# A hybrid decoder block in seven-product form: the output product's weights loaded and summed during the projections, and the attention branch's turned heads emptied a step ahead

## The chip, the cores and the metric
The kernel runs on one core of a Trainium2 chip. The metric is the device time of one execution in microseconds (us). Its engines are TensorE (PE in the profile, PEld its weight loads), VectorE (DVE), ScalarE (ACT), GpSimd (POOL) and SyncE (SP), which only issues DMAs here. Each engine works through its own instructions in the order in which they stand in the program, and waits on semaphores for the others.

## The reference, cut to what matters
One layer, 1024 positions, width 1024, all in float32. Two branches work on the normalised input and meet in gates; an MLP follows.

```python
h = rms_norm(x, g_mix)
z = h @ w_in                      # q1 q2 k1 k2 v | qr kr vr gr | gate_a gate_t
a = diff_attention(q1, q2, k1, k2, va, lam)            # 4 heads of 128
a = _rms(a, SUBLN_EPS) * g_diff_sub * (1 - lam_init)
r = _rms(retention(qr, kr, vr), ...) * silu(gr)        # 4 heads of 128
m = sigmoid(gate_a) * (a @ w_diff_proj) + sigmoid(gate_t) * (r @ w_ret_proj)
x = x + m @ w_out
u = causal_dwconv(rms_norm(x, g_ffn) @ w_up, conv_w, conv_b)
x = x + (silu(gate half of u) * (other half)) @ w_down
out = rms_norm(x, g_final)
```

The lines are shortened: shapes and reshapes are left out.

## The kernel before
**Numbers in two pieces.** Every float32 operand of a product is cut into an upper piece `hi` and a remainder `lo`, both fp32r: ScalarE makes `hi` (`copy`, line 291), VectorE makes `lo` (`sub`, line 285). One product of two such operands is three matmuls: hi with hi, hi with lo, lo with hi (`part`, line 276). A tile of a `Form` holds `hi` in its columns 0 to 511 and `lo` behind it.

**Seven products for eight.** A product of two matrices cut in four quadrants each is done with seven smaller products, of sums of quadrants. For the output product `wo` (`m @ w_out`) the parts run in the order 1, 6, 5, 7, 3, 4, 2. Each part goes over four k (128 rows of a quadrant) and, within a k, over four blocks d of 128 output channels, three matmuls for each k and d: 12 a k, 48 a part. Parts 1, 6, 7, 4 gather in one set of four PSUM banks (tag a), parts 5, 3, 2 in another (tag b). With u0, u1 the left and right half of a weight tile `wou` and v0, v1 those of `wov` (in the trace's names), the weight sides of the parts are: 1: u0; 6: S2 = v1 - S3; 5: S1 = u1 + v1; 7: S3 = u0 - u1; 3: v0 - S2; 4: v1; 2: v0. `Loaded.prepare` (line 1026) makes the sums, `Loaded.side` (line 1034) hands them out. Before, S3 is written over u0 and S1 over u1, just ahead of the parts that use them.

**The stages around the change.** In the program's order: the last gates (`gt`, a product of the normalised input, ending about 582 us); in their last steps the four heads of the attention's result `oa` are turned; the projection `pa` of the attention (eight weights `wpa`, 24 matmuls each); the projection `pr` of the retention (eight weights `wpr`, the same); the output product `wo`; the norm; the MLP's two products (`up`, `wd`).

**The steps.** The stages are written as a list of `Step`s, and `issue` (line 338) writes the program from it. At step i it issues the loads of step i + 9, the sums of step i + 4, the `hi` copies of step i + 3, the `lo` remainders of step i + 2, and then the step's own `pre` list, its matmuls `mm` and its `post` list (evictions and whatever was hung on the step):

```python
(0, lambda s: s.first), (LOAD, lambda s: s.load), (SUMS, lambda s: s.sums), (HI, ...),
(LO, ...), (0, lambda s: s.pre + [s.mm] + s.post),
```

`at_step(i, op)` hangs an operation on the end of step i's `post`; `load_with(i, op)` has a load issued during step i. The projections and `wo` stand in the order in which this writes them; `n_gates` is the number of steps up to the end of the gates, and every weight of `pa` and `pr` has two steps (its two halves of 512 columns).

**Turned heads.** `turn_a(h)` (line 795) transposes the eight 128 x 128 blocks of head h into two PSUM banks (`turned`, line 783, tag "b", two banks in all; `pta` in the trace). `finish_a(h)` empties them: two ScalarE copies for the upper piece (line 803), two VectorE operations for the remainder (line 805). Head h is turned at the end of step n_gates - 7 + h and was emptied at the end of the next step, behind that step's evictions. The next head's transposes, which need the same two banks, stand behind that.

**Projections.** `projection` (line 758) loads a weight `raw_pa` or `raw_pr` (SP's queue), splits it, and runs two steps of 12 matmuls. `times` (line 918) multiplies each half into the loaded gate (`ga_in`, `gt_in`; line 922, VectorE); `merge` (line 966) adds the two branches (line 288) and, for blocks 4 to 7, makes the three sums `t` and `ga_in` that the output product's activations need (line 285).

**Queues and tiles.** All loads here are issued by SP in one order (`Queue.load`, line 171: each is ordered behind the one before). SP waits at a load until the tile that it fills is free, and what is behind it waits too. Tiles come from tags with a fixed number of buffers each; a new tile takes the oldest buffer of its tag, once its last reader is done. Before, the sixteen quarter loads of `wo` (256 KB each) stand behind all loads of the projections, in the order u0, u1, v0, v1 over the four k, then the eight blocks of `x2` (the residual input), and `zg` and `zu` weights follow. `evict_wo` adds each part to `x2` (line 288) and each finished half is saved by another SP transfer.

Of the kernel before, what the change touches and what calls it, by code (L numbers as in the profile page):

```python
# [135 lines left out]
def hybrid_block(ctx: ExitStack, tc: tile.TileContext, units, xT, wall, lams, pars, consts, dist, out):  # L136
# [6 lines left out]
    def t4(tag, name, dt=F32, shape=(P, 1024)):  # L143
        return tp.tile(list(shape), dt, tag=tag, name=name, bufs=BUFS[tag])
# [35 lines left out]
    queue = Queue()  # L180
# [101 lines left out]
    HK = KB // 2  # L282

    def sub(out, a, b, engine=nc.vector):
        engine.tensor_tensor(out, a, b, op=ALU.subtract)  # L285

    def plus(out, a, b, engine=nc.vector):
        engine.tensor_tensor(out, a, b, op=ALU.add)  # L288
# [24 lines left out]
    def weight_form(src, name):  # L313
        n_forms[0] += 1
        return Form(("whi", "wlo")[n_forms[0] % 2], src, name)
# [10 lines left out]
    steps, index, behind = [], {}, []  # L326
# [23 lines left out]
    def manual():  # L350
        return tc.manual_schedule(engines={getattr(mybir.EngineType, n) for n in ("PE", "DVE", "Activation", "Pool")})

    with ExitStack() as first:
# [13 lines left out]
        u = []  # L367
        w = None
        for k in range(KB):
            xt = t4("s", f"x{k}")  # L370
            tag = "br" if k < 4 else "c" if k < 6 else "vo" if k < 7 else "s"
# [57 lines left out]
        for h in range(NH):  # L429
            for c in range(2):  # L430
                v = va[h][:, 4 * c : 4 * c + 4, :]
# [168 lines left out]
        class Pair:  # L600
# [20 lines left out]
            def add(self, p):  # L621
                side = {1: "a11", 2: "a12", 5: "a21", 6: "s2", 7: "a11", 3: "a12", 4: "a22"}[p]
                w = weight_form(lambda: getattr(self, side), f"w{self.label}_{p}")
                into_a = p in (1, 6, 7, 4)

# [115 lines left out]
        def at_step(i, *ops):  # L741
            steps[i].post.extend(ops)

        def load_with(i, *ops):

            steps[i + LOAD].load[:0] = ops

        def act_step(label, ps, w, acts, c, load=(), forms=(), post=()):

            cs = slice(c * 512, (c + 1) * 512)  # L750

            def mm():
                ps[c] = psum("gx", f"ps_{label}_{c}")
                part(ps[c], [(w.t, k * P) for k in range(NH)], [[t[:, cs] for t in acts[k]] for k in range(NH)], True, True)

            step((label, c), mm, load, (), forms, [partial(op, cs, lambda: ps[c]) for op in post])

        def projection(name, j, acts, load, done, behind=()):

            raw, ps = {}, {}  # L760

            def load_raw():
                raw[0] = t4("wraw", f"raw_{name}{j}")[:, 0:512]
                queue.load_unit(raw[0], (name, j))

            w = weight_form(lambda: raw[0], f"w{name}_{j}")
            for c in range(2):
                act_step(
                    f"{name}{j}", ps, w, acts, c, [load_raw, *load] if c == 0 else (), [w] if c == 0 else (),
                    [lambda cs, ps: done(cs, ps())],  # L770
                )
            steps[-1].post.extend(behind)
# [6 lines left out]
        def scale_heads(o, r):  # L779

            nc.vector.tensor_tensor(o, o, r.rearrange("p (a b) -> p a b", b=1).broadcast_to([P, 8, DV]), op=ALU.mult)
# [113 lines left out]
        n_gates = len(steps)  # L895
# [7 lines left out]
        for h in range(NH):  # L903
            at_step(18 + h, lambda h=h: scale_heads(oa[h], rstd_a[:, h * NST : (h + 1) * NST]))
            at_step(n_gates - 7 + h, partial(turn_a, h))
            at_step(n_gates - 6 + h, partial(finish_a, h))


        MERGED = ("br",) * 5 + ("s", "s", "vo")
# [8 lines left out]
        def times(t):  # L918


            def go(cs, ps):
                nc.vector.tensor_tensor(t()[:, cs], t()[:, cs], ps, op=ALU.mult)

            return go
# [32 lines left out]
        for n in range(2 * NH):  # L957
            h, c = n // 2, n % 2
# [16 lines left out]

        for j in (0, 4, 1, 5, 2, 6, 3, 7):
            projection("pr", j, rT, [partial(load_gate, j)], times(lambda j=j: gates[j]), [partial(merge, j)])
        with manual():
            issue(4)

# [39 lines left out]
    class Loaded(Resident):  # L1020
# [3 lines left out]
            return []  # L1024

        def prepare(self, p, k):
            if p == 6:
                self.sum2(k)
            if p == 5:
                self.sum1(k)  # L1030
            if p == 3:
                sub(self.s24[k], self.tiles[1][k][:, 0:512], self.s24[k])

        def side(self, p, k):
            u, v = (t[k] for t in self.tiles)
            s = self.s24.get(k)
            return {1: u[:, 0:512], 7: u[:, 0:512], 2: v[:, 0:512], 4: v[:, 512:], 6: s, 3: s, 5: u[:, 512:]}[p]

    class Streamed(Resident):

# [126 lines left out]
    tc.keep_in_program_order(nc.scalar.activation(table, eps_n, AF.Sqrt))  # L1167
    steps.clear()
    index.clear()
    wo = Loaded("wo", ["g", "wraw", "wraw", "h0"], ["h0"] * HK, "h0")  # L1170
    for q in (0, 2, 1, 3):
        for k in range(HK):
            wo.load(k, q)
    for d in range(KB):
        x2.append(t4("h1" if d < HK else "s", f"x2_{d}"))
        x2_saved.append(dram.tile([P, S], F32, name=f"x2_saved{d}"))
# [15 lines left out]
    def evict_first(p, d, ps, cols):  # L1192
# [8 lines left out]
    seven_parts(  # L1201
        "wo", (1, 6, 5, 7, 3, 4, 2), HK, wo, lambda p, k: [],
        lambda p, k: [partial(merged_sum4, k)] if p == 4 else [], merged_side,
        lambda p, k: "h0" if p == 1 and k < 2 else "c",
        evict_first, squared_wo, {p: (2, [slice(0, 512)]) for p in (3, 4, 2)},
    )

# [379 lines left out]
```

## Time and profile before

| | before |
|---|---|
| median of 3 runs | 1434.86 us (1434.17 to 1435.17) |
| profiled execution | 1434.84 us |
| its span | 1433.0 us |
| mean granted TensorE clock | 0.984 of full |
| TensorE busy | 1368.6 us, 96% |
| VectorE busy | 1068.0 us, 75% |
| ScalarE busy | 703.4 us, 49% |
| GpSimd busy | 154.3 us, 11% |

The span is that of the profiled execution, from its first instruction to its last; the time reported for it is 1.84 us longer. Busy times are sums over the whole span, so they say which engine is scarce, not where. Where time is lost is read from the waits and the timelines of single stretches: a row of a timeline is a run of like instructions with its start, its length and, in brackets, the idle time ahead of it and the operation of another engine that ended it. `PEclk` in a table of stretches is the granted TensorE clock as a share of full speed. Buffer numbers are left out of the names: `wpr` is any of the eight split weights of that name.

### The profile page before, as it was taken

To read this page: it belongs to the slowest core of one execution; us is meant where nothing else is said; L and a number is where in the kernel's file an instruction comes from. 1 tells how busy PE (TensorE), PEld (TensorE's weight loads), DVE (VectorE), ACT (ScalarE), POOL (GpSimd) and SP (SyncE) were. 2 spreads that over 40 slices of the span, in tenths; PEclk is the share of its full clock that TensorE was granted. 3 is DMA by queue.
4 is the path that set the end of the run, shared out by engine and by line. 5 is a ranking of instruction groups with operands and counts; after the bars stand their busy time and mean duration, and the time that the engine had idled before them with its cause. 6 is when DMAs were issued, how large, how long until landed. Compare 5 with 4: busy or idle time off the path is not lost.

```text
span 1433.0 us, 18055 instructions
## 1 busy us (share of the span) xinstructions
PE 1368.6 (96%) x6472; PEld 1134.0 (79%) x6472; DVE 1068.0 (75%) x1699; ACT 703.4 (49%) x1318; POOL 154.3 (11%) x92
## 2 busy tenths in 40 slices
PE   7899899989999998999998989999999999999996
PEld 7887788878888886788776767888888888888885
DVE  6759765675655553467968989888988899897876
ACT  6544665564454434221445465455555556444452
POOL 6711001000000000000000012111111112200000
PEclk9999999999999999999989999999999999999997
DMA  7313101314334332635324134434433365943223
GB/s 250 125 45 121 56 16 45 137 70 143 137 125 136 108 110 81 251 138 180 153 100 148 59 113 159 133 122 136 139 126 125 125 228 195 331 165 103 94 90 118
DMA packets 81018, 187.55 MB, mean 131 GB/s; under 512 B 8320, under 2 KB 18944, under 8 KB 80928
## 3 DMA queue, kind: packets, MB, share of 16 engines
q1 hardware_dynamic: 80736, 185.74, 37.8%
q8 instruction: 51, 0.84, 0.2%
q0 software_dynamic: 192, 0.66, 0.1%
q14 instruction: 39, 0.32, 0.1%
HBM read 136.81 MB, written 49.55 MB: 130 GB/s over the span
## 4 chain that ended last, share of the span: by engine, by line
PE 42%; DVE 7%; ACT 1%; issue 1%; DVEq 0%; ACTq 0%
PE up L276 24%; PE wd L276 14%; PE wo L276 4%; DVE wf L285 1%; DVE f L285 1%; DVE x L1461 1%; DVE y L1381 1%; DVE ssum L228 1%; DVE x L1230 1%; DVE x L288 1%; DVE x L285 0%; ACT f L291 0%; DVE zg L288 0%; DVE raw_zg L285 0%; DVE wwo L285 0%
## 5 line engine op out<-in xcount | busy, mean ns | idle before, releaser
L276 PE MATMUL up<-f,wf 128*128 128x512 f32 x1848 | 424.8, 391 | 9.2 <-DVE wf L285 3.4
L276 PEld LDWEIGHTS up<-f,wf 128*128 128x128 f32 x1848 | 345.3, 188 | 88.1 <-DVE wf L285 6.4
L276 PE MATMUL wd<-awd,wwd 128*128 128x512 f32 (+1 forms) x960 | 212.2, 383 | 0.0
L276 PEld LDWEIGHTS wd<-awd,wwd 128*128 128x128 f32 x960 | 176.0, 189 | 35.4 <-issue 0.5
L285 POOL TENSOR_TENSOR t12g<-y 128x512 f32<-128x512 f32 x11 | 19.8, 1796 | 673.3 <-DVE y L1391 538.4
L276 PE MATMUL wo<-awo,wwo 128*128 128x512 f32 x336 | 83.2, 407 | 7.4 <-DVE awo L285 7.1
L276 PEld LDWEIGHTS wo<-awo,wwo 128*128 128x128 f32 x336 | 64.9, 196 | 24.8 <-DVE awo L285 10.1
L512 ACT ACTIVATE s<-s,row 128x512 f32<-128x512 f32 (+7 forms) x64 | 49.5, 773 | 26.7 <-DVE row L507 26.2
L1381 DVE SCALAR_TENSOR_TENSOR y<-zg,par,y 128x1022 f32<-128x1022 f32 (+1 forms) x44 | 58.6, 1333 | 2.9 <-ACT y L1378 2.9
L502 PE MATMUL pss<-k,q 128*128 128x512 f32 (+2 forms) x192 | 52.8, 371 | 5.6 <-DVE row L507 5.5
L288 DVE TENSOR_TENSOR zg<-zg,up 128x512 f32<-128x512 f32 x44 | 30.2, 685 | 37.0 <-PE up L276 34.6
L1381 DVE SCALAR_TENSOR_TENSOR y<-zu,par,y 128x1022 f32<-128x1022 f32 (+1 forms) x44 | 56.1, 1277 | 0.0
L291 ACT ACTIVATE zg<-up 128x512 f32<-128x512 f32 x44 | 26.1, 596 | 58.5 <-PE up L276 58.5
L285 DVE TENSOR_TENSOR awd<-act_in,awd 128x512 fp32r<-128x512 f32 x77 | 53.7, 697 | 0.0
L507 DVE CUSTOM_DVE_ANT_0 s<-pss,dist_t 128x512 f32<-128x512 f32 (+3 forms) x64 | 37.0, 587 | 21.1 <-PE pss L502 19.7
L291 ACT ACTIVATE awd<-act_in 128x512 fp32r<-128x512 f32 x77 | 47.5, 616 | 0.3 <-DVE wf L285 0.2
L276 PE MATMUL ps_pa<-a,wpa 128*128 128x512 f32 x192 | 46.0, 394 | 0.0
L206 PE MATMUL psq<-hT,hi_q 128*128 128x512 f32 x128 | 43.2, 415 | 2.5 <-ACT hi_q L163 1.7
L291 ACT ACTIVATE zu<-up 128x512 f32<-128x512 f32 x44 | 26.2, 596 | 39.2 <-PE up L276 39.1
L276 PE MATMUL ps_pr<-r,wpr 128*128 128x512 f32 x192 | 43.7, 389 | 0.0
L291 ACT ACTIVATE wwd<-wdv 128x512 fp32r<-128x512 f32 x33 | 20.9, 632 | 46.1 <-PE wd L276 37.1
L530 PEld LDWEIGHTS po<-va,at 128*128 128x128 f32 x288 | 38.1, 195 | 6.2 <-ACT at L527 4.1
(367 smaller groups left out, 2822.9 us busy)
## 6 DMA issues: line engine op xcount, KB each, us to landing
act_in<-act SPq DMA_DIRECT2D x77, 256.0 KB, 2.9
act<-y SPq DMA_DIRECT2D x55, 256.0 KB, 2.2
raw_zg<-in_wall SPq DMA_DIRECT2D x22, 512.0 KB, 3.4
raw_zu<-in_wall SPq DMA_DIRECT2D x22, 512.0 KB, 4.1
x<-in_x SPq DMA_DIRECT2D x15, 512.0 KB, 7.8
act<-t12g SPq DMA_DIRECT2D x22, 256.0 KB, 2.0
wdu<-in_wall SPq DMA_DIRECT2D x22, 256.0 KB, 4.8
wdv<-in_wall SPq DMA_DIRECT2D x22, 256.0 KB, 5.7
```

The source lines that it names most:

```text
L206: nc.tensor.matmul(ps, w, a, start=i == 0, stop=i == n - 1)
L228: engine.tensor_tensor(self.ssum, self.ssum, sq, op=ALU.add)
L276: nc.tensor.matmul(ps[:, cols], w[:, x * 512 + at : x * 512 + at + P], a[y][:, cols], start=start and i == 0, stop=stop and i == n - 1, sk ...
L285: engine.tensor_tensor(out, a, b, op=ALU.subtract)
L288: engine.tensor_tensor(out, a, b, op=ALU.add)
L291: nc.scalar.activation(out, a, AF.Copy)
L502: nc.tensor.matmul(ps[:, : max(n, 256)], qs[m][:, i * P : (i + 1) * P], k[:, c : c + max(n, 256)], start=e == 0, stop=e == 1,)
L507: nc.vector.tensor_tensor_reduce(s[:, c : c + n], ps[:, :n], dst_t[:, S - width + c : S - width + c + n], SLOPES[h], low_, op0=ALU.add, op ...
L512: nc.scalar.activation(s[:, :width], s[:, :width], AF.Exp, bias=low_, scale=-1.0, accum_out=z[:, m : m + 1])
L530: nc.tensor.matmul(po, at[:, k * P : (k + 1) * P], va[h][:, kb, :], start=kb == 0, stop=kb == i)
L1230: nc.vector.scalar_tensor_tensor(y, y, gain(1, at), row, op0=ALU.mult, op1=ALU.mult)
L1381: nc.vector.scalar_tensor_tensor(y[side][:, n:], z[:, : S - n], t[:, j : j + 1], y[side][:, n:], op0=ALU.mult, op1=ALU.add)
```

## The change
Two things are changed.

First, `finish_a(h)` moves from the `post` list of its step to the `pre` list, so ScalarE's two copies and VectorE's two remainders of a head stand ahead of that step's matmuls and evictions instead of behind them.

Second, the output product's sixteen weight loads are issued during the projections (four in each of four pairs of steps from n_gates + 8 on), into tiles of tags that are free then; and the sums S3, S2 and S1 are made there too (`sums_wo(k)` at the end of steps n_gates + 23, 25, 27 and 29, which lie in `pr`), S2 and S3 into four tiles of their own. So u0 is no longer written over; part 7 reads S3's tile. `prepare` keeps only the sum for part 3. The activations' forms of `wo` all take tag "h0"; two later loads of the MLP's weights (`raw_zg2e`, `raw_zg3e`), which take tiles of the same tag, stand as a result behind the second saves of `x2` blocks 4, 5 and 6 in SP's queue instead of ahead.

```diff
--- before.py
+++ after.py
@@ -903,7 +903,7 @@
         for h in range(NH):
             at_step(18 + h, lambda h=h: scale_heads(oa[h], rstd_a[:, h * NST : (h + 1) * NST]))
             at_step(n_gates - 7 + h, partial(turn_a, h))
-            at_step(n_gates - 6 + h, partial(finish_a, h))
+            steps[n_gates - 6 + h].pre.append(partial(finish_a, h))
 
 
         MERGED = ("br",) * 5 + ("s", "s", "vo")
@@ -975,6 +975,32 @@
 
         for j in (0, 4, 1, 5, 2, 6, 3, 7):
             projection("pr", j, rT, [partial(load_gate, j)], times(lambda j=j: gates[j]), [partial(merge, j)])
+
+
+        wo_u, wo_v, wo_s2, wo_s3 = {}, {}, {}, {}
+
+        def load_wo(k, q):
+
+            tiles = (wo_u, wo_v)[q % 2]
+            if q < 2:
+                tag = "br" if q == 0 else "g" if k == 0 else "c"
+                tiles[k] = t4(tag, f"wo{'uv'[q]}{k}")
+            queue.load_unit(tiles[k][:, q // 2 * 512 : q // 2 * 512 + 512], ("wo", k, q))
+
+        def sums_wo(k):
+            u, v = wo_u[k], wo_v[k]
+            if k % 2 == 0:
+                for sums, n in ((wo_s2, 2), (wo_s3, 3)):
+                    t = t4("h0", f"wo_s{n}_{k}")
+                    sums[k], sums[k + 1] = t[:, 0:512], t[:, 512:]
+            sub(wo_s3[k], u[:, 0:512], u[:, 512:])
+            sub(wo_s2[k], v[:, 512:], wo_s3[k])
+            plus(u[:, 512:], u[:, 512:], v[:, 512:])
+
+        for k in range(HK):
+            for q in range(4):
+                load_with(n_gates + 8 + 2 * k + q // 2, partial(load_wo, k, q))
+            at_step(n_gates + 23 + 2 * k, partial(sums_wo, k))
         with manual():
             issue(4)
 
@@ -1024,17 +1050,12 @@
             return []
 
         def prepare(self, p, k):
-            if p == 6:
-                self.sum2(k)
-            if p == 5:
-                self.sum1(k)
             if p == 3:
-                sub(self.s24[k], self.tiles[1][k][:, 0:512], self.s24[k])
+                sub(wo_s2[k], wo_v[k][:, 0:512], wo_s2[k])
 
         def side(self, p, k):
-            u, v = (t[k] for t in self.tiles)
-            s = self.s24.get(k)
-            return {1: u[:, 0:512], 7: u[:, 0:512], 2: v[:, 0:512], 4: v[:, 512:], 6: s, 3: s, 5: u[:, 512:]}[p]
+            u, v, s = wo_u[k], wo_v[k], wo_s2[k]
+            return {1: u[:, 0:512], 7: wo_s3[k], 2: v[:, 0:512], 4: v[:, 512:], 6: s, 3: s, 5: u[:, 512:]}[p]
 
     class Streamed(Resident):
 
@@ -1167,10 +1188,7 @@
     tc.keep_in_program_order(nc.scalar.activation(table, eps_n, AF.Sqrt))
     steps.clear()
     index.clear()
-    wo = Loaded("wo", ["g", "wraw", "wraw", "h0"], ["h0"] * HK, "h0")
-    for q in (0, 2, 1, 3):
-        for k in range(HK):
-            wo.load(k, q)
+    wo = Loaded("wo", None, None, None)
     for d in range(KB):
         x2.append(t4("h1" if d < HK else "s", f"x2_{d}"))
         x2_saved.append(dram.tile([P, S], F32, name=f"x2_saved{d}"))
@@ -1201,7 +1219,7 @@
     seven_parts(
         "wo", (1, 6, 5, 7, 3, 4, 2), HK, wo, lambda p, k: [],
         lambda p, k: [partial(merged_sum4, k)] if p == 4 else [], merged_side,
-        lambda p, k: "h0" if p == 1 and k < 2 else "c",
+        lambda p, k: "h0",
         evict_first, squared_wo, {p: (2, [slice(0, 512)]) for p in (3, 4, 2)},
     )
 
```

ScalarE at the turn of heads 0 and 1 before (`pta` the turned head, `a` the emptied upper piece, `z_gt` the gate's eviction, `wgt` a weight's upper piece):

```order
L291 ACTIVATE wgt_3_4808<-raw_gt_4566 128x512
L619 ACTIVATE z_gt_4687<-pa_gt_4542 128x512
L619 ACTIVATE z_gt_4687<-z_gt_4687 128x512
L803 ACTIVATE a_4827<-pta_0_4798,gd 128x512
L803 ACTIVATE a_4827<-pta_1_4803,gd 128x512
L291 ACTIVATE wgt_7_4847<-raw_gt_4566 128x512
L291 ACTIVATE z_gt_4863<-pb_gt_4850 128x512
L803 ACTIVATE a_4865<-pta_0_4833,gd 128x512
L803 ACTIVATE a_4865<-pta_1_4838,gd 128x512
```

And now:

```order
L291 ACTIVATE wgt_3_4808<-raw_gt_4566 128x512
L803 ACTIVATE a_4811<-pta_0_4798,gd 128x512
L803 ACTIVATE a_4811<-pta_1_4803,gd 128x512
L619 ACTIVATE z_gt_4687<-pa_gt_4542 128x512
L619 ACTIVATE z_gt_4687<-z_gt_4687 128x512
L291 ACTIVATE wgt_7_4847<-raw_gt_4566 128x512
L803 ACTIVATE a_4850<-pta_0_4833,gd 128x512
L803 ACTIVATE a_4850<-pta_1_4838,gd 128x512
L291 ACTIVATE z_gt_4869<-pb_gt_4856 128x512
```

The two copies of head 0 have moved past the two sigmoids of `z_gt`, and those of head 1 past the eviction of `pb_gt`.

VectorE at the end of the projections before, from the evictions of one `wpr` block to those of the second next (`gt_in` the gate that is multiplied, `ga_in` the merged block, `t` its sums, `wpr` a weight's remainder):

```order
L922 TENSOR_TENSOR gt_in<-gt_in,ps_pr_1_5489 128x512
L288 TENSOR_TENSOR ga_in<-ga_in,gt_in 128x1024
L285 TENSOR_TENSOR t_1_5504<-ga_in 128x512
L285 TENSOR_TENSOR t_1_5504<-ga_in,t_1_5504 128x512
L285 TENSOR_TENSOR ga_in<-ga_in 128x512
L285 TENSOR_TENSOR wpr_5487<-raw_pr_5375,wpr_5487 128x512
L922 TENSOR_TENSOR gt_in<-gt_in,ps_pr_0_5509 128x512
L922 TENSOR_TENSOR gt_in<-gt_in,ps_pr_1_5525 128x512
L288 TENSOR_TENSOR ga_in<-ga_in,gt_in 128x1024
L285 TENSOR_TENSOR wpr_5523<-raw_pr_5411,wpr_5523 128x512
L922 TENSOR_TENSOR gt_in<-gt_in,ps_pr_0_5541 128x512
```

And now (`wo_s`, `wou`, `wov` are the output product's S3 and S2, u and v):

```order
L922 TENSOR_TENSOR gt_in<-gt_in,ps_pr_1_5513 128x512
L288 TENSOR_TENSOR ga_in<-ga_in,gt_in 128x1024
L285 TENSOR_TENSOR t_1_5528<-ga_in 128x512
L285 TENSOR_TENSOR t_1_5528<-ga_in,t_1_5528 128x512
L285 TENSOR_TENSOR ga_in<-ga_in 128x512
L285 TENSOR_TENSOR wo_s_0_5533<-wou_5157 128x512
L285 TENSOR_TENSOR wo_s_0_5532<-wov_5155,wo_s_0_5533 128x512
L288 TENSOR_TENSOR wou_5157<-wou_5157,wov_5155 128x512
L285 TENSOR_TENSOR wpr_5511<-raw_pr_5399,wpr_5511 128x512
L922 TENSOR_TENSOR gt_in<-gt_in,ps_pr_0_5538 128x512
L922 TENSOR_TENSOR gt_in<-gt_in,ps_pr_1_5554 128x512
L285 TENSOR_TENSOR wwo_0_5712<-wou_5157,wwo_0_5712 128x512
```

Three sums stand ahead of the sixth weight's remainder; the next three stand behind the next merge, ahead of the seventh's.

VectorE at the end of the last projection and the start of the output product before (`wwo`, `awo` the remainders of its weights and activations):

```order
L922 TENSOR_TENSOR gt_in<-gt_in,ps_pr_0_5577 128x512
L922 TENSOR_TENSOR gt_in<-gt_in,ps_pr_1_5591 128x512
L288 TENSOR_TENSOR ga_in<-ga_in,gt_in 128x1024
L922 TENSOR_TENSOR gt_in<-gt_in,ps_pr_0_5606 128x512
L285 TENSOR_TENSOR awo_0_5698<-ga_in,awo_0_5698 128x512
L285 TENSOR_TENSOR wwo_1_5700<-wou_5648,wwo_1_5700 128x512
L922 TENSOR_TENSOR gt_in<-gt_in,ps_pr_1_5620 128x512
L285 TENSOR_TENSOR awo_1_5702<-ga_in,awo_1_5702 128x512
L285 TENSOR_TENSOR wou_5646<-wou_5646 128x512
L288 TENSOR_TENSOR ga_in<-ga_in,gt_in 128x1024
L285 TENSOR_TENSOR t_3_5635<-ga_in 128x512
L285 TENSOR_TENSOR wos_0_5713<-wov_5658,wou_5646 128x512
```

And now:

```order
L285 TENSOR_TENSOR awo_0_5714<-ga_in,awo_0_5714 128x512
L285 TENSOR_TENSOR wwo_1_5716<-wou_5218,wwo_1_5716 128x512
L285 TENSOR_TENSOR awo_1_5718<-ga_in,awo_1_5718 128x512
L285 TENSOR_TENSOR wwo_2_5722<-wou_5279,wwo_2_5722 128x512
L285 TENSOR_TENSOR awo_2_5724<-ga_in,awo_2_5724 128x512
L288 TENSOR_TENSOR ga_in<-ga_in,gt_in 128x1024
L285 TENSOR_TENSOR wo_s_2_5609<-wou_5340 128x512
L285 TENSOR_TENSOR wwo_3_5728<-wou_5340,wwo_3_5728 128x512
L285 TENSOR_TENSOR wo_s_2_5608<-wov_5338,wo_s_2_5609 128x512
L288 TENSOR_TENSOR wou_5340<-wou_5340,wov_5338 128x512
L922 TENSOR_TENSOR gt_in<-gt_in,ps_pr_0_5646 128x512
L922 TENSOR_TENSOR gt_in<-gt_in,ps_pr_1_5660 128x512
```

The remainders of the first part's first three k now stand ahead of the last merges instead of among them, the fourth k's sums among them instead of behind, and the multiplication of the last `pr` block behind those sums.

## Rows read from the trace of the kernel before

**Rows 1.** Waits of TensorE: waiter <- releaser: us, count, longest us.

```profile
PE pta L787 <- DVE a L805: 6.7, 3, 2.6
```

**Rows 2.** TensorE's timeline, 546 to 590: start us, length us, operation, idle before.

```profile
550.30 1.03 PE L787 MATMUL pta<-cst,oa 128*128 128x128 f32 x8
551.09 3.01 PE L276 MATMUL pa_gt<-ht,wgt 128*128 128x512 f32 x12
556.67 1.77 PE L787 MATMUL pta<-cst,oa 128*128 128x128 f32 x8 [2.57 <-DVE a L805]
...
564.40 1.31 PE L787 MATMUL pta<-cst,oa 128*128 128x128 f32 x8 [2.05 <-DVE a L805]
...
579.62 3.01 PE L276 MATMUL pa_gt<-ht,wgt 128*128 128x512 f32 x12 [0.78 <-DVE z_gt L288]
```

**Rows 3.** ScalarE's and VectorE's timeline in the same stretch.

```profile
554.14 0.60 ACT L619 ACTIVATE z_gt<-pa_gt 128x512 f32<-128x512 f32 x1 [2.96 <-PE pa_gt L276]
...
555.15 1.26 ACT L803 ACTIVATE a<-pta,gd 128x512 fp32r<-128x512 f32 x2
555.87 1.41 DVE L805 SCALAR_TENSOR_TENSOR a<-pta,gd,a 128x512 fp32r<-128x512 f32 x2 [4.08 <-ACT a L803]
...
576.75 1.40 DVE L805 SCALAR_TENSOR_TENSOR a<-pta,gd,a 128x512 fp32r<-128x512 f32 x2
```

**Rows 4.** Six stretches: length us, busy by engine, PEclk, DMA share, GB/s.

```profile
556.00:562.00 6.00, 5.33 (x20) 4.25 (x20) 1.87 (x3) 0.93 (x2) 0.00 (x0) 0.72 0.22 87
562.00:570.00 8.00, 4.41 (x22) 2.99 (x20) 2.30 (x4) 3.77 (x7) 0.00 (x0) 1.00 0.34 108
620.00:640.00 20.00, 20.00 (x93) 16.55 (x92) 13.36 (x21) 4.73 (x8) 0.00 (x0) 1.00 0.37 119
680.00:690.00 10.00, 7.54 (x31) 5.27 (x30) 9.73 (x16) 5.15 (x10) 0.00 (x0) 1.00 1.04 412
734.00:748.00 14.00, 12.19 (x38) 9.94 (x39) 8.58 (x16) 4.96 (x12) 0.00 (x0) 0.63 0.10 37
748.00:760.00 12.00, 10.83 (x45) 7.92 (x43) 9.73 (x16) 8.55 (x16) 0.00 (x0) 1.00 0.32 101
```

**Rows 5.** TensorE's timeline, 590 to 740, last projections and output product.

```profile
631.19 43.68 PE L276 MATMUL ps_pr<-r,wpr 128*128 128x512 f32 x192
674.71 5.83 PE L276 MATMUL wo<-awo,wwo 128*128 128x512 f32 x25
682.09 3.06 PE L276 MATMUL wo<-awo,wwo 128*128 128x512 f32 x12 [1.55 <-DVE awo L285]
685.70 2.79 PE L276 MATMUL wo<-awo,wwo 128*128 128x512 f32 x11 [0.55 <-DVE awo L285]
688.84 44.06 PE L276 MATMUL wo<-awo,wwo 128*128 128x512 f32 x193 [0.35 <-ACT first_part L291]
735.81 4.64 PE L276 MATMUL wo<-awo,wwo 128*128 128x512 f32 x10 [2.92 <-DVE awo L285]
```

**Rows 6.** VectorE's timeline, 650 to 682.

```profile
653.15 0.69 DVE L922 TENSOR_TENSOR gt_in<-gt_in,ps_pr 128x512 f32<-128x512 f32 x1 [2.03 <-PE ps_pr L276]
653.88 1.22 DVE L288 TENSOR_TENSOR ga_in<-ga_in,gt_in 128x1024 f32<-128x1024 f32 x1
655.02 0.68 DVE L285 TENSOR_TENSOR t<-ga_in 128x512 f32<-128x512 f32 x1
655.74 0.69 DVE L285 TENSOR_TENSOR t<-ga_in,t 128x512 f32<-128x512 f32 x1
...
656.95 0.68 DVE L285 TENSOR_TENSOR wpr<-raw_pr,wpr 128x512 fp32r<-128x512 f32 x1
...
680.14 0.69 DVE L285 TENSOR_TENSOR wos<-wov,wou 128x512 f32<-128x512 f32 x1 [1.60 <-DMA wov<-in_wall]
```

**Rows 7.** Timeline of all engines, 728 to 800: an eviction and a load's reader.

```profile
754.15 0.68 DVE L288 TENSOR_TENSOR x<-x,wo 128x512 f32<-128x512 f32 x1
...
774.59 0.61 ACT L291 ACTIVATE wf<-raw_zg3e 128x512 fp32r<-128x512 f32 x1
```

## The prediction

> **What bounds the kernel now.** I read the views in this order. First the waits of TensorE: the turning of the attention's heads into `pta` has waited 6.7 us for VectorE in three waits, the longest 2.6 us [rows 1]. Then TensorE's timeline around these three places, where the reader is to see an almost gapless stream that stops three times and restarts [rows 2]; the timeline of ScalarE and VectorE there, for who is late and why [rows 3]; the granted clock by stretches [rows 4]; and last TensorE and VectorE at the end of the gated projections and the start of the output product [rows 5, 6]. TensorE sets the end in all of this: over the eight `wpr` weights it runs 192 matmuls in 43.68 us, 0.2275 us each, without a wait [rows 5]. So a microsecond counts only where TensorE waits, or where a late VectorE newly makes it wait.
>
> **Part one: the turned heads.** Each head's transposes fill two banks of `pta`, and the next head's need the same two. Before, ScalarE's copies of head 0 (555.15) stand behind the two sigmoids of a block of `pa_gt` (the first at 554.14), which wait for the step's own twelve matmuls; VectorE's lower halves come at 555.87 and take 1.41 [rows 3]. TensorE, done with its twelve matmuls at about 553.8, begins the next head at 556.67, after 2.57 us marked as waiting for VectorE's `a`; then 2.05 at 564.40; and a third time likewise [rows 2].
> With the copies ahead of the step's evictions they hang on the transposes alone, which end about 551.3 (550.30 + 1.03). Two copies take 1.26, a lower half 0.69 to 0.72 behind its copy, so the second lower half ends at about 553.2, before 553.8. In the second and third turn ScalarE first has the eviction of the step before, and the last lower half comes about 0.1 us after the transposes that want its bank: I leave 0.2 for both. The copies now run under matmuls; the fourth head's lower halves did that already and took 1.40 for two (576.75), as much as the 1.41 beside a waiting TensorE [rows 3], so that costs nothing.
> The path from 551.09 to 579.62 is 28.53 us [rows 2]. New: five groups of twelve matmuls, 60 x 0.2275 = 13.65; three sets of transposes at 0.79 (550.30 to 551.09), 2.37; the 0.78 us wait for `z_gt`, which stays, since it is the eviction between two parts of one bank; and the 0.2. That is 17.0, a gain of 11.5 us. 6.7 of it are the three waits. The rest is mostly clock: after the first wait the granted clock is 0.72 of full from 556 to 562, in part the 1.2 GHz level, while it is 1.00 from 562 to 570, across the second wait [rows 4].
> The bounds: 6.7, if the clock falls all the same, and 11.7, if not even the 0.2 is left. I take 11.5, as the new stream has no wait above 0.8 there, and the row with waits of about that size (748 to 760, 1.00) shows no fall [rows 4]. What follows, loads included, waits for TensorE's and VectorE's progress and moves with it.
>
> **Part two: the output product's weights.** Sixteen loads of 256 KB move from behind the last projection into four groups among the `raw_pr` and `gt_in` loads of SP's queue. No tile that they take is freed later than the end of the gates (about 582), so SP is not held by them. The traffic: 119 GB/s there now, plus four loads in each 5.46 us, 192 GB/s, is 311; the busiest stretch ran 412 [rows 4]. I cost that at nothing; the cover is that a weight's load is issued some ten microseconds before TensorE wants it, and if it went, VectorE's lower half would come late as below. Gone is VectorE's wait for `wov` of 1.60 [rows 6].
> VectorE's twelve sums (three for each of four k) are no fewer, only earlier: each group takes 0.60 + 0.72 + 0.60 = 1.92 us (0.60 from start to start, 0.72 where one reads the other [rows 6]). They stand ahead of lower halves that TensorE wants soon, and there the working goes down VectorE's queue from 653.15, times in the frame of before:
> - The lower half of the sixth weight started at 656.95 [rows 6]; with one group ahead it starts at 658.87 and ends at 659.55. TensorE is at that weight at 631.19 + 5 x 5.46 = 658.5 and wants it at its third matmul, 658.95: a wait of 0.6.
> - From there to the eighth weight's lower half VectorE has 18 steps without a pause: 12 of 0.60, three of 0.72, two of 1.14 (behind a 1024-wide sum), one of 0.73 [rows 6], 12.4 in all: it starts at 671.25 and ends at 671.93. TensorE wants it at 658.5 + 0.6 + 2 x 5.46 + 0.45 = 670.5: a wait of 1.5. The projections end at 677.0 instead of 674.8.
> - Thirteen more steps (12 of 0.60, one of 1.14) bring VectorE to the eviction of the eighth block's first half, which starts at 679.6 and ends at 680.3. That bank is the output product's fourth; TensorE is there after nine matmuls, at 679.0: a wait of 1.3. The 39 matmuls left of the first part take 8.87: the second part starts at 689.2, against 688.84 [rows 5].
> So the three waits at the start of the output product (1.55, 0.55 and 0.35, 2.45 together [rows 5]) go, and waits of 3.4 stand a little earlier: a loss of 0.4 us. Bounds: 3.2 us of gain (before lost 14.13 - 48 x 0.2275 there, if no moved sum is on the path) and 7.7 us of loss (all twelve on it: four times 1.92). I take the loss of 0.4, since the chain has a row for every step.
> Behind this VectorE is lighter by the same sums, which buys nothing: TensorE runs 688.84 to 733 without a wait, and the wait of 2.92 at 735.81 [rows 5] is for halves that stand behind evictions of its own last blocks, in the same order now. The activations' pieces now all use the tag h0, so the loads `raw_zg2e` and `raw_zg3e` are issued behind the saves of `x` instead of ahead: `raw_zg3e` waits for the block evicted at 754.15, and is first read at 774.59 [rows 7], so 20 us cover one load of 512 KB. Cost: nothing.
>
> **Sum.** 1434.84 (the profiled execution, which is the median of 1434.86 within 0.02) - 11.5 + 0.4 = 1423.7 us.
>
> **Rivals.**
> - *The output product's start gains as well.* VectorE keeps up, and the lost 3.2 us there go too: 1434.84 - 11.5 - 3.2 = 1420.1. For it: VectorE is idle for 2.03 us ahead of 653.15 [rows 6]. Against: no step of the chain above is a guess, and the idle time lies ahead of the first sum. Chance 0.10.
> - *The stretch at the lower clock after 735.81 changes.* From 734 to 748 the clock is 0.63 [rows 4]; (1 - 0.63) x 12.19 busy us is 4.5 us that a full clock would save. Everything arrives 11 us earlier, and the stretch could be shorter, down to 1423.7 - 4.5 = 1419.2, or longer by as much as the 1.7 us (0.28 x 6) that one fall costs after the first turn, 1425.4. For it: two waits of 2.05 and 2.57 had different outcomes. Against: the runs before agree within 1.0 us. Chance 0.12. The Trainium skill (TensorE: Matmul & The Clock Gate, section "What's actually happening") says that the chip judges activity in windows that run free of the kernel. By that rule a wait's place decides whether it costs clock; the two waits agree with it.
> - *The turns still wait,* behind the evictions of the step before, or the clock falls there all the same: a gain of 6.7 only, 1434.84 - 6.7 + 0.4 = 1428.5. Chance 0.06.
> - *Slower: the clock goes down in the projections.* The new waits of 0.6, 1.5 and 1.3 follow each other in 20 us where there was no wait. If TensorE fell to 1.2 GHz at the first and stayed there until the second part at 689, its matmul work of about 30 us would take twice as long: 1423.7 + 30 = 1454. It decides for slower than before from 11 us of such work on. For it: each fall in [rows 4] followed a wait. Against: from 748 to 760, with a wait of 1.14 and a smaller one in about 9 us, the clock stays at 1.00 [rows 4]. Chance 0.03. The Trainium skill (same page, section "A second HAM failure mode: psum-queue depth-cycling") tells of a kernel whose short waits for banks made the clock go up and down. No stretch of the trace before shows that.
> - *It doesn't do what it says:* the earlier copies find their tiles still being stored or loaded, and the time is 1434.8. The stores of these tiles' former contents are issued before 540, so 0.03.
>
> **Numbers.** The forecast, 1423.7, has 0.66, with its own range of 1421.5 to 1425.7 (the chain on VectorE by one microsecond and a half, the turns by one). The range for 8 in 10 reaches into the first two rivals and a little towards the third: 1419.8 to 1427.0. About 0.2% (2.9 us) can be told from no change. Faster by more: 0.66 + 0.10 + 0.12 + 0.06 = 0.94; within: 0.03; slower: 0.03.
>
> **What would show it.** Right: `pta` waits for `a` under 0.3 us in all, the granted clock at 1.00 where it was 0.72, and the first `ps_pa` matmul 11 us earlier; waits of TensorE for `wpr` at the sixth and eighth weight and inside the first part for `gt_in`, together 3 to 4 us; the wait of 2.9 for `awo` still there. Wrong: waits for `raw_pr` or `raw_zg3e`, a clock below 1.00 in the projections, or no wait for `wpr` at all (then VectorE's chain is mis-sized).

## The result, and the profile after

Over six runs each the changed kernel takes 1423.36 us (1420.29 to 1429.49), the kernel before 1435.01 (1431.19 to 1439.53): a ratio of 0.9925, 95% interval 0.9897 to 0.9954. The forecast was 1423.7, in a range of 1419.8 to 1427.0. The profiled execution of the changed kernel took 1421.57, its span is 1419.8 and its mean clock 0.988, against 1434.84, 1433.0 and 0.984 before.

TensorE's timeline through the four turned heads (start us, length us, operation, idle before, as in [rows 2]):

```profile
551.13 1.03 PE L787 MATMUL pta<-cst,oa 128*128 128x128 f32 x8
551.92 3.01 PE L276 MATMUL pa_gt<-ht,wgt 128*128 128x512 f32 x12
554.77 1.03 PE L787 MATMUL pta<-cst,oa 128*128 128x128 f32 x8
...
558.39 1.04 PE L787 MATMUL pta<-cst,oa 128*128 128x128 f32 x8
...
562.03 1.03 PE L787 MATMUL pta<-cst,oa 128*128 128x128 f32 x8
...
569.30 3.01 PE L276 MATMUL pa_gt<-ht,wgt 128*128 128x512 f32 x12 [0.78 <-DVE z_gt L288]
```

Not one of the transposes waits; the only bracket left is the eviction between two parts of one bank. From the second group of twelve matmuls to the last, 28.53 us before [rows 2], it is now 569.30 - 551.92 = 17.38. VectorE's remainders of a head against the same clock:

```profile
552.62 1.41 DVE L805 SCALAR_TENSOR_TENSOR a<-pta,gd,a 128x512 fp32r<-128x512 f32 x2
...
557.22 1.41 DVE L805 SCALAR_TENSOR_TENSOR a<-pta,gd,a 128x512 fp32r<-128x512 f32 x2 [2.58 <-ACT a L803]
```

The first head's are done at 554.03, 0.74 before the next transposes; the second's at 558.63, 0.24 after the next ones have begun with the other bank. They took 1.41 beside a waiting TensorE [rows 3] and take 1.41 beside a running one. The two stretches that answer to the first two of [rows 4] (the eighth number of a line is the granted clock):

```profile
556.00:562.00 6.00, 6.00 (x32) 4.97 (x31) 3.69 (x6) 4.03 (x8) 0.00 (x0) 1.00 0.36 122
562.00:570.00 8.00, 7.22 (x36) 5.80 (x35) 3.71 (x6) 3.85 (x6) 0.00 (x0) 1.00 0.63 201
```

The 0.72 has gone with the waits. Then TensorE from the last projections to the norm, which answers to [rows 5]:

```profile
648.55 11.17 PE L276 MATMUL ps_pr<-r,wpr 128*128 128x512 f32 x48 [0.61 <-DVE wpr L285]
660.93 5.28 PE L276 MATMUL ps_pr<-r,wpr 128*128 128x512 f32 x22 [1.21 <-DVE wpr L285]
666.05 2.20 PE L276 MATMUL wo<-awo,wwo 128*128 128x512 f32 x9
669.46 52.90 PE L276 MATMUL wo<-awo,wwo 128*128 128x512 f32 x232 [1.21 <-DVE gt_in L922]
725.28 4.22 PE L276 MATMUL wo<-awo,wwo 128*128 128x512 f32 x11 [2.92 <-DVE awo L285]
...
754.90 0.73 PE L276 MATMUL up<-f,wf 128*128 128x512 f32 x2 [0.56 <-ACT wf L291]
```

Three waits of 0.61, 1.21 and 1.21 stand where there was none, and the three at the start of the output product (1.55, 0.55, 0.35) are gone. VectorE beside the first of them shows what stands ahead of the weight's remainder that TensorE waits for, three sums:

```profile
645.89 0.68 DVE L285 TENSOR_TENSOR wo_s<-wou 128x512 f32<-128x512 f32 x1
646.60 0.69 DVE L285 TENSOR_TENSOR wo_s<-wov,wo_s 128x512 f32<-128x512 f32 x1
647.21 0.68 DVE L288 TENSOR_TENSOR wou<-wou,wov 128x512 f32<-128x512 f32 x1
...
647.82 0.68 DVE L285 TENSOR_TENSOR wpr<-raw_pr,wpr 128x512 fp32r<-128x512 f32 x1
```

Stage by stage, the two profiles differ by 13.2 us: the start of the turns comes 0.8 later (the programs are alike up to there), the turns take 11.15 less, the way from the last `pa_gt` group to the second part 0.2 less (109.22 before; now 669.46 plus the 39 matmuls left, 8.87, is 678.33, so 109.03), from there to the first matmul of `up` 2.0 less, and the rest 0.7 less. Two rows of before belong to this, a wait for one of the retention's heads ahead of the projection `pr`, and the first matmul of `up`:

```profile
606.21 0.44 PE L787 MATMUL ptr<-cst,or 128*128 128x128 f32 x2 [0.68 <-DVE or L781]
...
767.38 0.73 PE L276 MATMUL up<-f,wf 128*128 128x512 f32 x2 [0.32 <-ACT wf L291]
```

### The profile page after: what moved, and what is told of

The parts are those of the page before. It is cut to its first block, busy times and chain, and to the rows that moved or that the text cites. A ratio compares the mean times of both kernels' runs of the same rounds, so it can differ in the third digit from the quotient of the medians.

```text
span 1419.8 us, 18040 instructions
## 1 busy us (share of the span) xinstructions
PE 1361.2 (96%) x6472; PEld 1129.9 (80%) x6472; DVE 1067.8 (75%) x1699; ACT 702.7 (49%) x1318; POOL 154.4 (11%) x92
## 4 chain that ended last, share of the span: by engine, by line
PE 78%; DVE 13%; issue 3%; ACT 3%; POOL 1%; DMA 1%; SPq 0%; DVEq 0%; ACTq 0%; POOLq 0%
PE up L276 24%; PE wd L276 14%; PE wo L276 4%; PE pa_gt L276 3%; PE pa_ga L276 3%; PE ps_pa L276 3%; PE psq L206 3%; PE psk L206 2%; PE pb_ga L276 2%; PE pb_gt L276 2%; PE ps_pr L276 2%; PE pss L502 2%; PE po L530 2%; PE psqr L206 2%; PE pa_gr L276 2%
## 5 line engine op out<-in xcount | busy, mean ns | idle before, releaser
L276 PEld LDWEIGHTS ps_pr<-r,wpr 128*128 128x128 f32 x192 | 35.8, 188 | 10.1 <-DVE wpr L285 2.8
```

The costliest lines, as they stand in the source:

```text
L276: nc.tensor.matmul(ps[:, cols], w[:, x * 512 + at : x * 512 + at + P], a[y][:, cols], start=start and i == 0, stop=stop and i == n - 1, sk ...
```

## The experiments

Whole times of one and the same kernel spread by up to 9 us here, and part of that arises ahead of the turns: in the profiles of the kernels below, which do the same up to there, the group of matmuls behind the first turned head starts at anything between 550.7 and 557.2. So the verdicts rest on stages within one profile: the **turns** (second group of twelve to last `pa_gt` group), the **seam** (last `pa_gt` group to the second part of the output product, whose start is worked out from the row before at 0.2275 us a matmul where no row begins there) and the **tail of the product** (from there to the first matmul of `up`). Changed kernel: 17.38, 109.03 and 76.57; kernel before: 28.53, 109.22 and 78.54.

**Only the turns.**

```diff
-            at_step(n_gates - 6 + h, partial(finish_a, h))
+            steps[n_gates - 6 + h].pre.append(partial(finish_a, h))
```

(on the kernel before)

> The kernel before with only the four turned heads emptied ahead of their step's evictions. Theory: the whole gain is here. The three waits of pta are gone, the granted clock is 1.00 through the turns, and the stretch from the second group of matmuls beside the turns to the last pa_gt group takes 17.4 us instead of 28.53; everything behind runs as before, with waits of 1.55, 0.55 and 0.35 at the start of the output product. Time 11.2 us below before, about 1423.7. Rival (the output product's part gives some 2 us of the 13.2 that the two profiles differ by): 9 us below before, about 1426, with the stretch at the lower clock after the wait of 2.92 as long as before (10 us).

1422.91 us, a ratio of 0.993 (0.9912 to 0.9948) to before. The turns take 17.39. The product's tail takes 76.64, with a short stretch at the lower clock, so the stretch is short here without the weights' part too. The seam, though, takes 108.01 and not 109.22, mostly since the first wait at the start of the product is 0.52 now:

```profile
672.11 3.04 PE L276 MATMUL wo<-awo,wwo 128*128 128x512 f32 x12 [0.52 <-DVE awo L285]
675.72 2.79 PE L276 MATMUL wo<-awo,wwo 128*128 128x512 f32 x11 [0.57 <-DVE awo L285]
```

VectorE's wait for `wov` there is 0.57 in this profile, 1.60 before [rows 6]:

```profile
670.16 0.69 DVE L285 TENSOR_TENSOR wos<-wov,wou 128x512 f32<-128x512 f32 x1 [0.57 <-DMA wov<-in_wall]
```

The whole gain can be had with this one line; against it, the weights' part costs 1.0 us at the seam, by one profile of each.

**Only the weights.** The changed kernel with `at_step(n_gates - 6 + h, partial(finish_a, h))` back in place.

> The changed kernel with the turned heads emptied behind the evictions again, as before. Theory: no change against before beyond 1 us, 1434 to 1436: the waits of 0.61 and 1.21 for wpr and 1.21 for gt_in stand in place of 0.68 for the retention's head and of 1.55, 0.55 and 0.35 at the start of the output product, so TensorE begins the second part 109.0 us after the last pa_gt group, against 109.2 before. Rival (the early weights and sums save what the profiles differ by beyond the turns): 1432.5 or less.

1436.96 us, a ratio of 1.0015 (1.0003 to 1.0028): if anything slower. The stages are 28.51, 109.08 and 76.26, the same three waits of 0.61, 1.20 and 1.21 at the seam. The theory's stage times hold, the rival's gain isn't there; the 3 us by which the median lies above before aren't in these stages, and where they come from stays open. In this profile the second group of twelve begins 5.6 us later than before (556.67 against 551.09), and all that follows is 2.9 shorter. The turns' waits are those of before to 0.01 us, and yet the slow matmuls don't follow the same ones: here the first and the second (twelve in 4.59 and 4.17), before the first and the third (twelve in 4.26 and 4.17). Before:

```profile
558.10 4.26 PE L276 MATMUL pb_gt<-hT,wgt 128*128 128x512 f32 x12
...
571.94 4.17 PE L276 MATMUL pb_gt<-hT,wgt 128*128 128x512 f32 x12
```

Here, behind the second wait and behind the third:

```profile
569.96 1.77 PE L787 MATMUL pta<-cst,oa 128*128 128x128 f32 x8 [2.05 <-DVE a L805]
571.38 4.17 PE L276 MATMUL pa_gt<-ht,wgt 128*128 128x512 f32 x12
577.61 1.31 PE L787 MATMUL pta<-cst,oa 128*128 128x128 f32 x8 [2.05 <-DVE a L805]
578.67 3.01 PE L276 MATMUL pb_gt<-hT,wgt 128*128 128x512 f32 x12
```

**One wait left in the turns, then two others.**

```diff
-            steps[n_gates - 6 + h].pre.append(partial(finish_a, h))
+            (steps[n_gates - 6 + h].post if h == 0 else steps[n_gates - 6 + h].pre).append(partial(finish_a, h))
```

and the same with `h in (1, 2)`.

> The changed kernel with head 0 alone emptied behind its step's evictions, as before; heads 1 to 3 stay ahead. Theory (a wait of some 2.6 us is followed by about 4 us at half clock): the wait of 2.57 ahead of the second head's transposes is back, the granted clock falls to half for some 3.8 us behind it, and the time is 2.6 + 1.9 = 4.5 us above the changed kernel. Rival (the clock fell because three waits followed each other): the wait alone, 2.6 us, and a clock of 1.00.

> The changed kernel with heads 1 and 2 emptied behind their step's evictions, as before; heads 0 and 3 stay ahead. Theory (a wait of 2 us or more is followed by half clock for some 4 us or not at all, whatever stands around it): two waits of 2.05 are back, 4.1 us, and one or both are followed by a stretch at half clock of about 2 us' cost each, so the stretch from the second group beside the turns to the last pa_gt group takes 17.4 + 4.1 + 2 to 4 = 23.5 to 25.5 us. Rival (the clock needs a wait of more than 2.1 us, or a row of three, to fall): 21.5 us and a clock of 1.00.

With the first wait alone the turns take 574.14 - 552.19 = 21.95, 4.57 above the changed kernel: 2.57 of wait and 2.0 of slower matmuls behind it (the median, 1429.68, is 6.3 above). One wait is enough for the clock to fall:

```profile
557.73 1.53 PE L787 MATMUL pta<-cst,oa 128*128 128x128 f32 x8 [2.57 <-DVE a L805]
558.92 4.48 PE L276 MATMUL pb_gt<-hT,wgt 128*128 128x512 f32 x12
```

With two of 2.05 they take 23.82 (median 1432.4), 6.44 more: 4.1 of waits and 2.3 of clock, behind the first of the two and not behind the second:

```profile
563.56 1.77 PE L787 MATMUL pta<-cst,oa 128*128 128x128 f32 x8 [2.05 <-DVE a L805]
564.98 4.08 PE L276 MATMUL pa_gt<-ht,wgt 128*128 128x512 f32 x12
571.12 1.32 PE L787 MATMUL pta<-cst,oa 128*128 128x128 f32 x8 [2.05 <-DVE a L805]
572.19 3.01 PE L276 MATMUL pb_gt<-hT,wgt 128*128 128x512 f32 x12
```

Both theories held, both rivals fell.

**The same sums, in VectorE's gaps.**

```diff
-            at_step(n_gates + 23 + 2 * k, partial(sums_wo, k))
+            at_step(n_gates + (16, 18, 22, 26)[k], partial(sums_wo, k))
```

> The changed kernel with each group of three sums moved to an earlier step, behind the eviction of the first half of the first, second, fourth and sixth pr block, where VectorE was idle for 2.03 us. Theory (the three new waits come from the sums ahead of the lower halves): the waits of 0.61 and 1.21 for wpr and of 1.21 for gt_in vanish or shrink to under 0.3 each, and the second part of the output product starts 2.4 to 3.0 us earlier: about 1420.6. Rival (the waits come from late loads, or VectorE is short of time there whatever the order): they stay, or come back at other weights, within 1 us of the changed kernel.

1422.46 us. The seam takes 106.05, 2.98 less than in the changed kernel: two of the three waits are gone, and 0.45 is left at the eighth weight, behind the last group of sums.

```profile
664.59 5.30 PE L276 MATMUL ps_pr<-r,wpr 128*128 128x512 f32 x22 [0.45 <-DVE wpr L285]
669.73 54.79 PE L276 MATMUL wo<-awo,wwo 128*128 128x512 f32 x241
```

So the waits came from the sums' places; the loads are in time. The medians, 0.9 us apart, can't tell as much.

**Early loads without early sums.** `prepare` of the changed kernel makes the sums again, S3 and S2 in tiles of their own:

```diff
-            at_step(n_gates + 23 + 2 * k, partial(sums_wo, k))
...
         def prepare(self, p, k):
+            if p == 6:
+                sums_wo(k)
+            if p == 5:
+                plus(wo_u[k][:, 512:], wo_u[k][:, 512:], wo_v[k][:, 512:])
```

(shortened: `sums_wo` loses its last line, which `prepare` now has for part 5, and `side` looks the sums up once they exist)

> The changed kernel with the output product's weights loaded early, but the sums S3, S2 and S1 made where the kernel before made them, ahead of parts 6 and 5 (S3 and S2 still in tiles of their own). Theory (early loads take away VectorE's waits for wov; early sums where they stood cost the waits for wpr): no wait for wpr, at the start of the output product waits of about 1 us in all, and TensorE begins the second part 107 to 108 us after the last pa_gt group, against 109.0 in the changed kernel and 108.0 where only the turns were changed. Rival (VectorE is short of time at the start of the output product whenever the sums stand there, loads early or late): waits of 2 us and more there, 109 us or more.

1424.18 us. The seam takes 105.30, less than either theory gave: neither a `wpr` nor the product's start waits.

```profile
568.08 3.01 PE L276 MATMUL pa_gt<-ht,wgt 128*128 128x512 f32 x12 [0.78 <-DVE z_gt L288]
...
618.92 43.70 PE L276 MATMUL ps_pr<-r,wpr 128*128 128x512 f32 x192
662.46 54.79 PE L276 MATMUL wo<-awo,wwo 128*128 128x512 f32 x241
720.17 3.88 PE L276 MATMUL wo<-awo,wwo 128*128 128x512 f32 x11 [2.92 <-DVE awo L285]
```

Against before (109.22) the loads alone gain 3.9 at the seam, against the kernel with only the turns changed (108.01) 2.7; the sums where the change put them cost 3.7. VectorE's order moved as well: the first `awo` remainder stands at 649.33 now, among the projections' evictions, so at the seam the order isn't that of the text alone, as the part on the kernel said, and what the loads and this order each give isn't parted. The gain isn't in the median, which lies 0.8 above the changed kernel's, and why is not shown. The profiled execution is the fastest of the five (1419.56), although the product's tail takes 79.45 in it, with the clock at the lower level for most of twelve microseconds behind the wait of 2.92:

```profile
720.00:724.00 4.00, 3.83 (x11) 2.56 (x11) 3.72 (x7) 3.21 (x6) 0.00 (x0) 0.70 0.18 69
724.00:728.00 4.00, 3.24 (x13) 2.90 (x13) 3.19 (x6) 1.01 (x5) 0.00 (x0) 0.50 0.16 62
728.00:732.00 4.00, 4.00 (x11) 3.13 (x10) 0.00 (x0) 0.56 (x2) 0.00 (x0) 0.52 0.00 0
```

**The wait of 2.92.** The four sums of part 4's activations made ahead of part 7:

```diff
-        lambda p, k: [partial(merged_sum4, k)] if p == 4 else [], merged_side,
+        lambda p, k: [partial(merged_sum4, k)] if p == 7 else [], merged_side,
```

> The changed kernel with the four sums of part 4's activations (the remaining sums t in VectorE's row ahead of the wait of 2.92 at 725) made four steps ahead of part 7 instead of part 4. Theory (that wait is VectorE's: three of the four sums, 1.9 us, stand ahead of the halves that TensorE waits for): the wait of 2.92 becomes about 1.0, and with a wait that short the clock does not fall behind it; gain 1.9 us of wait and some 2 us of clock, 4 us below the changed kernel in the stretch from part 6 to the first matmul of up. Rival (the halves wait for ScalarE's copies or for the evictions, not for the sums): the wait stays above 2, and nothing is gained.

1423.45 us: no gain. The wait shrank as expected, to 1.16, but the norm's column sums `row_f` (line 250), which stand next on TensorE, now wait 1.85 for the last squares instead of 0.42, and a stretch at the lower clock follows that (thirteen matmuls in 4.82). The tail takes 76.13, 0.4 less.

```profile
724.92 2.79 PE L276 MATMUL wo<-awo,wwo 128*128 128x512 f32 x11 [1.16 <-DVE awo L285]
729.56 1.05 PE L250 MATMUL row_f<-cst,ssum 128*128 128x1 f32 x8 [1.85 <-DVE ssum L228]
730.47 4.82 PE L276 MATMUL wo<-awo,wwo 128*128 128x512 f32 x13
```

The theory named the right engine and not the next wait in its queue.

**Both, and then the norm a step later.** The next kernel has that edit and the sums in steps `(16, 18, 20, 22)[k]`; the last one, beside that:

```diff
-    ahead_of(("wo", 4, 1), norm1.column)
-    ahead_of(("wo", 4, "d", 0, 1), norm1.across, norm1.keep)
+    ahead_of(("wo", 4, "d", 0, 0), norm1.column)
+    ahead_of(("wo", 4, "d", 0, 2), norm1.across, norm1.keep)
...
-    spread(("wo", 4, "d", 0, 1), ("wo", 2, 1), normal_sides(1, 1, 1))
+    spread(("wo", 4, "d", 0, 2), ("wo", 2, 1), normal_sides(1, 1, 1))
```

> The changed kernel with both edits: the groups of three sums behind the first halves of the first four pr blocks, and the sums of part 4's activations ahead of part 7. Theory: no wait for wpr or gt_in above 0.2 (3.0 us gained), the wait of 2.92 about 1.0 and no half clock behind it (4 us): 7 us below the changed kernel, about 1416. Rival: the wait of 0.45 for the eighth weight stays, or one comes back at the third or fourth weight, and the clock still falls: 1419 to 1421.

> The kernel with both edits (sums behind the first halves of the first four pr blocks, sums of part 4's activations ahead of part 7), and the norm's column sums row_f issued one step later, its spread over the rows two blocks later. Theory (row_f stands ahead of ready matmuls and waits 1.85 for the last squares): that wait is gone or under 0.3, the matmuls of part 4 run on, and part 6 to the first matmul of up takes 72.5 us instead of 74.4; about 1418. Rival (what is normalised later comes late for the first parts of up, or the halves of part 4's later blocks come late): a wait of 1 to 2 us appears there or at up, and the time stays at 1419.7.

The first of the two takes 1419.68 us (four runs, as for the second), a ratio of 0.9904 (0.9891 to 0.9918) to before. Its seam is 105.31, without any wait; its tail 74.39, with the waits of 1.16 and 1.85 and, this time, no lower clock behind them. The time is the rival's, 1419 to 1421, but neither of the rival's reasons holds. Against the changed kernel the seam gains 3.7 and the tail 2.2, 5.9 of the theory's 7; the theory had no term for the wait of `row_f`, which is 1.4 longer than in the changed kernel. The medians are 3.7 apart.

```profile
622.62 43.71 PE L276 MATMUL ps_pr<-r,wpr 128*128 128x512 f32 x192
666.17 54.79 PE L276 MATMUL wo<-awo,wwo 128*128 128x512 f32 x241
722.11 2.79 PE L276 MATMUL wo<-awo,wwo 128*128 128x512 f32 x11 [1.16 <-DVE awo L285]
726.75 1.05 PE L250 MATMUL row_f<-cst,ssum 128*128 128x1 f32 x8 [1.85 <-DVE ssum L228]
```

The second takes 1415.67, a ratio of 0.9869 (0.9848 to 0.9889). `row_f` doesn't wait, the tail is 73.35; the theory gave 72.5. Part of what it saves comes back as its rival said: the wait for the first weight of `up` is 1.78 instead of 0.33, and the first longer run of `up` matmuls takes 6.63 where the kernel without the last edit took 5.32 for as many (the granted clock from 750 to 754 is 0.57; in the kernel without it, it stays at 1.00).

```profile
719.77 5.51 PE L276 MATMUL wo<-awo,wwo 128*128 128x512 f32 x23 [1.16 <-DVE awo L285]
725.11 0.95 PE L250 MATMUL row_f<-cst,ssum 128*128 128x1 f32 x8
...
748.10 0.73 PE L276 MATMUL up<-f,wf 128*128 128x512 f32 x2 [1.78 <-ACT wf L291]
750.53 6.63 PE L276 MATMUL up<-f,wf 128*128 128x512 f32 x22 [1.70 <-DVE wf L285]
```

This is the fastest version of the study, some 19 us below before and 8 below the changed kernel. But of the 4.0 us between the last two medians only 1.0 shows in the tail, and 1.3 are lost again right behind it; where the rest comes from is not shown.

## Why the prediction was right, step by step

**The number.** That the median lies 0.3 us from the forecast is in part luck: by the interval the gain is anything from 6.6 to 14.8 us. What can be held against the working are the stages.

**The turns.** 11.5 forecast, 11.15 measured in the profile, 10.8 between medians where only they were changed. The new path took 17.38 and not 17.0: the five groups of twelve took 2.82 to 2.88 us each where the sum had 2.73, 0.6 in all, and the 0.2 for late remainders wasn't needed. Waits and clock had about the sizes that the sum gave them: taken back in two portions, a wait of 2.57 costs 4.57 and two of 2.05 cost 6.44, 11.0 together. That the clock would not fall in the new stream held. The two places where the last remainder comes a little late for its bank showed no wait at all.

**The clock, in the rival on the stretch after 735.81.** It had a chance of 0.12, as a shift by the earlier arrival. It rather differs from execution to execution: the tail took 76.57, 76.26, 78.86 and 76.33 in the profiles of changed, only the weights, the first turn late and the two later turns late, which have the same instructions there, and 78.54, 76.64, 76.40 and 79.45 in those of before, only the turns, the sums in the gaps and only the loads, all with that wait of 2.92 or one of 3.25. Some 2 us of the 13.2 between the two profiles are of that size, and can't be put down to the change; the medians, 11.65 apart, have such differences on both sides. That equal waits differ in what follows them agrees with the Trainium skill (TensorE: Matmul & The Clock Gate, section "What's actually happening"), by which the chip's windows run free of the kernel.

**The clock, in the rival that is slower.** Through the three new waits the granted clock stayed at 1.00 (645 to 673). But the sentence that no stretch of the trace before shows short waits making the clock go up and down was wrong. In the attention, from 144 to 152, TensorE has five waits of 0.58 to 0.90 close behind each other, the first three (0.72, 0.90 and 0.58) for VectorE's reading of a bank of `pss` (line 507), and the clock falls there:

```profile
144.00:148.00 4.00, 1.92 (x9) 1.14 (x8) 4.00 (x16) 3.64 (x13) 0.00 (x0) 0.97 0.39 157
148.00:152.00 4.00, 2.42 (x8) 1.73 (x9) 3.94 (x13) 2.24 (x6) 0.00 (x0) 0.50 0.33 133
```

TensorE is busy for 1.92 and 2.42 of four microseconds there, against 24.97 of 28 from 645 to 673. So the rival had a case in the trace, and its chance of 0.03 was given without it.

**The weights.** The sum had a loss of 0.4 from waits of 0.6, 1.5 and 1.3 in place of 2.45. Measured are 0.61, 1.21 and 1.21, at the weights and the bank that were named, and 0.2 us less for the seam as a whole. These are idle times, counted from the modelled end of the matmul before; from start to start, at 0.2275 a matmul, the three places lose 0.66 (620.13 to 648.55, 122 matmuls), 1.46 (648.55 to 660.93, 48) and 1.36 (666.05 to 669.46, nine), which is what the chain on VectorE gave. By that measure before lost 3.2 where its idle times sum to 2.45. Two things were off. The working left out a wait of 0.68 us for the retention's heads (`or`, line 781), which the changed kernel hasn't got; without it the seam would have lost 0.5. And the wait for `wov` isn't a constant of the kernel before: with only the turns changed it is 1.0 us shorter, and against that the weights' part loses 1.0. Whether the turns shortened it, or it varies from one execution to the next, isn't shown. The wait of 2.92 was read as one behind VectorE's evictions alone; with part 4's sums made earlier it shrank to 1.16, so 1.76 of it were sums.

**The bounds.** The end of the range "if no moved sum is on the path", 3.2 us of gain, is what the kernel with early loads alone shows: 3.9, 0.7 of it the retention's wait. So the small sum of the second part is a gain and a loss that cancel: the loads, with the order that came with them, are worth 3.9 us against before (2.7 against the turns alone), and three sums at a time ahead of a remainder that is due cost 3.7.

**Costed at nothing.** The loads: TensorE and VectorE never wait for `raw_pr`, `wou` or `wov`, with 273 GB/s from 610 to 626, where I had 311. `raw_zg3e`, issued at 742.53 behind the saves, is read at 761.84 without a wait for it.

## What to carry to other kernels

A read of a PSUM bank belongs where it hangs on its producer alone: behind an eviction that waits for later matmuls it makes the next user of the bank wait for these too, and the clock may add to the price, here 4.57 us for a wait of 2.57. Work that is moved forward to relieve a stage should go into gaps that the timeline shows on its engine, and not ahead of the next operand that is due; early loads and early sums are two edits, to be tried apart. Where a wait is taken away, the next instruction in that engine's queue is the one to price: here, of 1.76 us gained at one matmul, 1.43 came back at the next.

## What the runs showed of the hardware that was not expected

Whether the clock falls behind a wait of TensorE can't be read from the wait. Of waits of 2.05 us in the turns some were followed by a stretch at the lower clock, which took twelve matmuls from 3.0 to 4.2 us, and others, at the same place of another profile, were not. Waits of 1.16 and 1.85 us one behind the other were followed by such a stretch in one profile and not in another. In the tail of the product one such stretch cost, as an estimate, from 1.3 us (the changed kernel, 724 to 730: 0.71, 2.00 and 1.58 busy us at granted clocks of 0.74, 0.50 and 0.91) to 4.7 (the three rows with the loads alone), each busy time by what its clock lacks to 1.00. Differences below 3 us between kernels could therefore be settled within single stages only.
